# A contrast kernel on one core: the first tile loaded in two pieces instead of three, and stored as one DMA instead of two

## The chip, the cores and the metric

The kernel runs on one core of one Trainium2 chip. The metric is the device time of one execution in microseconds (us), given as the median of several runs. A profile is one more execution, recorded by the hardware profiler; its span runs from the first to the last instruction.

## What is computed

Sixteen images of three 512 x 512 channels in 32-bit floats: 48 channel planes of 262,144 pixels. Each plane is pushed away from its own mean by a factor of 1.5 and clipped.

```
mean = np.mean(x, axis=(2, 3), keepdims=True)
return np.clip(mean + factor * (x - mean), 0, 1).astype(np.float32)
```

With the factor a constant this is `factor * x + (1 - factor) * mean`, clipped to 0 and 1. The input has 50.33 MB, the output as much, so 100.66 MB must cross between HBM and the core's memory.

## The kernel before

**Tiles.** The planes lie one after another in HBM and are cut into rows of 16,384 floats (`ROW`, 64 KB). A tile has 128 such rows, one for each partition, so it holds eight planes of sixteen rows each and 8.39 MB; there are six tiles. The core's memory holds three at a time, in `ring` (L74): tile t lies in slot t mod 3, is worked on in place and stored from there. So tile 3 can be loaded only when tile 0 has been stored, tile 4 after tile 1, tile 5 after tile 2.

**One tile's work** (`compute`, L92). First the sums of the rows, in `add` (L82): VectorE (DVE) reduces the first 4,352 columns (`SUM`) at L85, and ScalarE (ACT) runs over the other 12,032 at L89, copying each element onto itself and accumulating. Then TensorE multiplies these partial sums with `blockw` (L100), a 128 x 128 matrix with (1 - factor) / 262,144 wherever two rows belong to one plane; the result, in `bias`, is the shift of each row. The matmul reads the DVE part and the ACT part one after the other and adds them up; one call in the source is two matmul instructions. Then two passes of DVE: multiply by the factor and add the shift (L103), clip below and above (L106). Then the store (L80).

**Tile 0 is special.** It is loaded in three column pieces: 2,048 columns (`SHORT`, 8 KB of each row), then up to column 8,192 (`HALF`, 24 KB of each row), then the other half (32 KB of each row). Its sums are taken for each half by itself, with 4,352 columns on DVE and 3,840 on ACT in each. Its two DVE passes and its store are cut at column 2,048: the first 8 KB of each row are finished and stored, then the other 56 KB.

**Order.** The order in which each engine gets its instructions is that of the source (`manual_schedule`, L111 to L125): the loads of tiles 0, 1 and 2, the work on tiles 0, 1 and 2 with each one's stores, the loads of tiles 3, 4 and 5, the work on these. Engines run beside each other and wait for data by semaphores. All DMAs are issued by SyncE (SP), which does nothing else, in this order; an issue that must wait holds up those behind it. All DMAs go through one queue that sixteen DMA engines serve, and each row of a DMA is one packet: an engine gets 8 packets of each of these 128-row DMAs, and one small packet that reports completion.

Of the kernel before, what the change touches and what calls it, by code (L numbers as in the profile page):

```python
# [1 line left out]

# [4 lines left out]


P = 128  # L10
ROW = 16384
HALF = ROW // 2
BUFS = 3
SHORT = 2048
SUM = 4352


@with_exitstack
def kernel(
    ctx: ExitStack,  # L20
    tc: tile.TileContext,
    x: bass.AP,
    factor: float,
    out: bass.AP,
):

    nc = tc.nc
    f32 = mybir.dt.float32  # L30
    Alu = mybir.AluOpType
    Act = mybir.ActivationFunctionType

    B, C, H, W = x.shape
    n_img, n_pix = B * C, H * W
    ppi = n_pix // ROW
    per_tile = P // ppi
    n_tiles = n_img // per_tile
    assert ppi * ROW == n_pix and per_tile * n_tiles == n_img

    factor = float(factor)
    wconst = (1.0 - factor) / float(n_pix)

    x_f = x.rearrange("b c h w -> (b c h w)")
    out_f = out.rearrange("b c h w -> (b c h w)")

    def dram(ap, t, c0=0, c1=ROW):
        return bass.AP(tensor=ap.tensor, offset=t * P * ROW + c0, ap=[[ROW, P], [1, c1 - c0]])

    consts = ctx.enter_context(tc.tile_pool(name="consts", bufs=1))  # L50
    xpool = ctx.enter_context(tc.tile_pool(name="xpool", bufs=1))
    small = ctx.enter_context(tc.tile_pool(name="small", bufs=1))
    psum = ctx.enter_context(tc.tile_pool(name="psum", bufs=1, space=bass.MemoryType.PSUM))


    sums = small.tile([P, 4 * n_tiles], f32, name="sums")
    bias = psum.tile([P, n_tiles], f32, name="bias")

    blockw = consts.tile([P, P], f32, name="blockw")
    blocks = blockw.rearrange("p (a b) -> p a b", b=ppi)  # L60
    nc.gpsimd.memset(blockw, wconst)  # L61
    for base, step in ((0, -ppi), (ppi - 1, ppi)):
        nc.gpsimd.affine_select(  # L63
            out=blocks,
            in_=blocks,
            compare_op=Alu.is_ge,
            fill=0.0,
            base=base,
            pattern=[[step, per_tile], [0, ppi]],
            channel_multiplier=1 if step < 0 else -1,  # L70
        )


    ring = xpool.tile([P, BUFS, ROW], f32, name="ring")  # L74

    def load(t, c0=0, c1=ROW):
        nc.sync.dma_start(out=ring[:, t % BUFS, c0:c1], in_=dram(x_f, t, c0, c1))  # L77

    def store(t, c0=0, c1=ROW):
        nc.sync.dma_start(out=dram(out_f, t, c0, c1), in_=ring[:, t % BUFS, c0:c1])  # L80

    def add(t, col, c0, c1, c2):  # L82
        xt = ring[:, t % BUFS, :]
        own = sums[:, 4 * t + col : 4 * t + col + 2]
        nc.vector.tensor_reduce(  # L85
            out=own[:, 0:1], in_=xt[:, c0:c1], axis=mybir.AxisListType.X, op=Alu.add
        )
        part = xt[:, c1:c2]
        nc.scalar.activation(out=part, in_=part, func=Act.Copy, accum_out=own[:, 1:2])  # L89
        return [own[:, 1:2], own[:, 0:1]]  # L90

    def compute(t, *cuts):  # L92
        xt = ring[:, t % BUFS, :]
        if t == 0:
            parts = add(t, 0, 0, SUM, HALF) + add(t, 2, HALF, HALF + SUM, ROW)
        else:
            parts = add(t, 0, 0, SUM, ROW)
        shift = bias[:, t : t + 1]
        for k, part in enumerate(parts):
            nc.tensor.matmul(shift, blockw, part, start=k == 0, stop=k == len(parts) - 1)  # L100
        for c0, c1 in zip((0, *cuts), (*cuts, ROW)):
            part = xt[:, c0:c1]
            nc.vector.tensor_scalar(  # L103
                out=part, in0=part, scalar1=factor, scalar2=shift, op0=Alu.mult, op1=Alu.add
            )
            nc.vector.tensor_scalar(  # L106
                out=part, in0=part, scalar1=0.0, scalar2=1.0, op0=Alu.max, op1=Alu.min
            )
            store(t, c0, c1)

    with tc.manual_schedule():  # L111
        load(0, 0, SHORT)
        load(0, SHORT, HALF)
        load(0, HALF, ROW)
        load(1)
        load(2)
        compute(0, SHORT)
        compute(1)
        compute(2)
        load(3)  # L120
        load(4)
        load(5)
        compute(3)
        compute(4)
        compute(5)  # L125


# [1 line left out]
_INS = ['x', 'factor']  # L129
_OUTS = [((16, 3, 512, 512), 'float32')]  # L130

_NUMBERS = {'factor': 1.5}


# [26 lines left out]
```

## Time and profile before

| | |
|---|---|
| time, median of 3 runs | 239.36 us (239.26 to 239.4) |
| span of the profiled execution | 237.3 us |
| DMA packets, bytes | 2160, 100.66 MB |
| DVE busy | 137.4 us |
| ACT busy | 59.9 us |
| tile 0 sums start (first half, second half) | 12.94 us, 22.58 us |
| tiles 1, 2 have arrived (ACT starts on them) | 41.93 us, 62.40 us |
| stores of tile 0 issued | 30.52 us, 45.83 us |
| stores of tiles 1, 2 issued | 71.00 us, 93.82 us |
| loads of tiles 3, 4, 5 issued | 94.24 us, 101.08 us, 120.82 us |
| tiles 3, 4, 5 have arrived | 139.79 us, 159.21 us, 178.57 us |
| stores of tiles 3, 4, 5 issued | 168.97 us, 191.81 us, 214.64 us |

The profiled execution's own device time is not recorded beside its span; the median of the timed runs lies 239.36 - 237.3 = 2.06 us above it, for what happens before the first and after the last instruction.

In the lines of the profile, L is a line of the kernel, "out<-in" the names of what an instruction writes and reads, and x a count. DVE is VectorE, ACT ScalarE, PE TensorE, SPq the queue of SyncE. The row named DMA has one digit for each of 40 equal slices of the span: the busy share of the sixteen DMA engines in tenths, 9 for 90% or more. A packet counts where it starts, so in a narrow window the share can be far above 1 and in the next one 0.

### The profile page before, as it was taken

How to read it: one execution, taken by the hardware profiler on the slowest of the kernel's cores; microseconds unless marked ns; L12 is line 12 of the kernel's file. 1: busy time of each engine (PE TensorE's matmuls, PEld its weight loads, DVE VectorE, ACT ScalarE, POOL GpSimd, SP SyncE). 2: the span in 40 equal slices, each digit the busy share in tenths (PEclk: the TensorE clock that was granted, in tenths of full speed). 3: DMA queues.
4: the chain of work that ended last, by engine and by line, in shares of the span. 5: the costliest groups of instructions: out<-in, count | busy, mean ns of one | idle time of the engine just before them, and what ended most of it. 6: DMA issues, size and time to landing. Idle time of an engine off the chain costs nothing.

```text
span 237.3 us, 186 instructions
## 1 busy us (share of the span) xinstructions
PE 7.9 (3%) x28; PEld 6.9 (3%) x28; DVE 137.4 (58%) x21; ACT 59.9 (25%) x15; POOL 1.1 (0%) x7
## 2 busy tenths in 40 slices
PE   0010100010001000000000000100000000000000
PEld 0010100010001000000000000100000000000000
DVE  0071899949998998000000043499989998991000
ACT  2051300980492000000000049319509800000000
POOL 1000000000000000000000000000000000000000
DMA  7999989899799798989899998989899998989894
GB/s 289 418 442 442 530 353 530 353 486 398 331 464 454 341 530 353 530 353 519 365 442 442 398 486 353 530 354 530 353 475 409 431 453 376 508 353 530 353 530 177
DMA packets 2160, 100.66 MB, mean 424 GB/s; under 512 B 240, under 2 KB 240, under 8 KB 240
## 3 DMA queue, kind: packets, MB, share of 16 engines
q1 hardware_dynamic: 2160, 100.66, 98.7%
HBM read 50.33 MB, written 50.33 MB: 424 GB/s over the span
## 4 chain that ended last, share of the span: by engine, by line
DVE 43%; DMA 36%; ACT 9%; PE 2%; SPq 1%; issue 0%; DVEq 0%; ACTq 0%
DMA ring<-in_x_dram 36%; DVE ring L103 18%; DVE ring L106 18%; ACT ring L89 9%; DVE sums L85 6%; PE bias L100 2%; SPq L77 1%; SPq L80 0%; DVEq L103 0%; ACTq L89 0%
## 5 line engine op out<-in xcount | busy, mean ns | idle before, releaser
L89 ACT ACTIVATE ring<-ring 128x12032 f32<-128x12032 f32 (+1 forms) x7 | 58.0, 8280 | 128.2 <-DMA ring<-in_x_dram 128.2
L85 DVE TENSOR_REDUCE sums<-ring 128x1 f32<-128x4352 f32 x7 | 32.8, 4683 | 63.9 <-DMA ring<-in_x_dram 63.9
L103 DVE TENSOR_SCALAR ring<-ring,bias 128x16384 f32<-128x16384 f32 (+2 forms) x7 | 52.8, 7538 | 12.9 <-PE bias L100 12.9
L106 DVE TENSOR_SCALAR ring<-ring 128x16384 f32<-128x16384 f32 (+2 forms) x7 | 52.3, 7476 | 0.2
L100 PE MATMUL bias<-sums,blockw 128*128 128x1 f32 x28 | 7.9, 360 | 189.1 <-ACT ring L89 175.4
L100 PEld LDWEIGHTS bias<-sums,blockw 128*128 128x128 f32 x28 | 6.9, 314 | 190.0 <-ACT ring L89 159.4
L89 ACT ACT_TABLE_LOAD x1 | 1.3, 1283 | 0.8 <-PEq L142 0.8
L89 ACT ACTIVATION_READ_ACCUMULATOR ring<-ring 128x1 f32 x7 | 1.3, 187 | 0.0
L63 POOL TENSOR_SCALAR_AFFINE_SELECT blockw<-blockw 128x128 f32<-128x128 f32 x2 | 0.7, 340 | 0.1
L61 POOL MEMSET blockw<- 128x128 f32 x1 | 0.2, 204 | 0.3 <-POOLq L142 0.3
L142 POOL MEMSET const-bfloat16-1.0<- 128x1 bf16 x1 | 0.1, 102 | 0.0
L142 POOL MEMSET const-uint8-127<- 128x1 uint8 x1 | 0.1, 102 | 0.0
L142 POOL MEMSET const-float32-0.0<- 128x1 f32 x1 | 0.1, 98 | 0.3 <-issue 0.3
L142 POOL MEMSET const-float32-1.0<- 128x1 f32 x1 | 0.1, 98 | 0.0
## 6 DMA issues: line engine op xcount, KB each, us to landing
out_dram<-ring SPq DMA_DIRECT2D x1, 7168.0 KB, 35.9
ring<-in_x_dram SPq DMA_DIRECT2D x1, 4096.0 KB, 20.8
ring<-in_x_dram SPq DMA_DIRECT2D x1, 3072.0 KB, 11.6
ring<-in_x_dram SPq DMA_DIRECT2D x1, 1024.0 KB, 4.7
out_dram<-ring SPq DMA_DIRECT2D x1, 1024.0 KB, 34.3
ring<-in_x_dram SPq DMA_DIRECT2D x5, 57.7
out_dram<-ring SPq DMA_DIRECT2D x5, 27.0
```

What stands on the lines that cost most here:

```text
L61: nc.gpsimd.memset(blockw, wconst)
L63: nc.gpsimd.affine_select(out=blocks, in_=blocks, compare_op=Alu.is_ge, fill=0.0, base=base, pattern=[[step, per_tile], [0, ppi]], channel ...
L77: nc.sync.dma_start(out=ring[:, t % BUFS, c0:c1], in_=dram(x_f, t, c0, c1))
L85: nc.vector.tensor_reduce(out=own[:, 0:1], in_=xt[:, c0:c1], axis=mybir.AxisListType.X, op=Alu.add)
L89: nc.scalar.activation(out=part, in_=part, func=Act.Copy, accum_out=own[:, 1:2])
L100: nc.tensor.matmul(shift, blockw, part, start=k == 0, stop=k == len(parts) - 1)
L103: nc.vector.tensor_scalar(out=part, in0=part, scalar1=factor, scalar2=shift, op0=Alu.mult, op1=Alu.add)
L106: nc.vector.tensor_scalar(out=part, in0=part, scalar1=0.0, scalar2=1.0, op0=Alu.max, op1=Alu.min)
L142: nc = _bacc.Bacc("TRN2", target_bir_lowering=False, num_devices=1)
```

## The change

Tile 0 is loaded in two pieces, its two column halves (32 KB of each row each). Its sums are taken as in every other tile: DVE over columns 0 to 4,351, ACT over the other 12,032, which need both halves. Its two DVE passes run over whole rows, and its store is one DMA of whole 64 KB rows. The other tiles keep their instructions, and the order of loads, work and stores stays the same; it is now written as a loop over groups of three tiles. `sums` shrinks from four columns for each tile to two.

```
-    def add(t, col, c0, c1, c2):
+    def add(t, c0, c1, c2):
...
-    def compute(t, *cuts):
+    def compute(t):
         xt = ring[:, t % BUFS, :]
-        if t == 0:
-            parts = add(t, 0, 0, SUM, HALF) + add(t, 2, HALF, HALF + SUM, ROW)
-        else:
-            parts = add(t, 0, 0, SUM, ROW)
+        parts = add(t, 0, SUM, ROW)
...
-        for c0, c1 in zip((0, *cuts), (*cuts, ROW)):
-            part = xt[:, c0:c1]
-            nc.vector.tensor_scalar(
-                out=part, in0=part, scalar1=factor, scalar2=shift, op0=Alu.mult, op1=Alu.add
-            )
-            nc.vector.tensor_scalar(
-                out=part, in0=part, scalar1=0.0, scalar2=1.0, op0=Alu.max, op1=Alu.min
-            )
-            store(t, c0, c1)
+        nc.vector.tensor_scalar(
+            out=xt, in0=xt, scalar1=factor, scalar2=shift, op0=Alu.mult, op1=Alu.add
+        )
+        nc.vector.tensor_scalar(
+            out=xt, in0=xt, scalar1=0.0, scalar2=1.0, op0=Alu.max, op1=Alu.min
+        )
 
     with tc.manual_schedule():
-        load(0, 0, SHORT)
-        load(0, SHORT, HALF)
-        load(0, HALF, ROW)
-        load(1)
-        load(2)
-        compute(0, SHORT)
-        compute(1)
-        compute(2)
-        load(3)
-        load(4)
-        load(5)
-        compute(3)
-        compute(4)
-        compute(5)
+        for first in range(0, n_tiles, BUFS):
+            turn = range(first, min(first + BUFS, n_tiles))
+            for t in turn:
+                if t == 0:
+                    load(t, 0, HALF)
+                    load(t, HALF, ROW)
+                else:
+                    load(t)
+            for t in turn:
+                compute(t)
+                store(t)
```

More of the change, by code (lines that the diff above doesn't have):

```diff
@@ L11 @@
 ROW = 16384
+BUFS = 3
+SUM = 4352
 HALF = ROW // 2
-BUFS = 3
-SHORT = 2048
-SUM = 4352
 @with_exitstack
@@ L53 @@
     psum = ctx.enter_context(tc.tile_pool(name="psum", bufs=1, space=bass.MemoryType.PSUM))
-    sums = small.tile([P, 4 * n_tiles], f32, name="sums")
+    sums = small.tile([P, 2 * n_tiles], f32, name="sums")
     bias = psum.tile([P, n_tiles], f32, name="bias")
@@ L80, in store @@
         nc.sync.dma_start(out=dram(out_f, t, c0, c1), in_=ring[:, t % BUFS, c0:c1])
-    def add(t, col, c0, c1, c2):
+    def add(t, c0, c1, c2):
         xt = ring[:, t % BUFS, :]
-        own = sums[:, 4 * t + col : 4 * t + col + 2]
+        own = sums[:, 2 * t : 2 * t + 2]
         nc.vector.tensor_reduce(
```

## The prediction

> **What bounds the kernel now.** I read the page first, for the share of each engine, then the DMA slices.
>
> ```profile
> span 237.3 us, 186 instructions
> PE 7.9 (3%) x28; PEld 6.9 (3%) x28; DVE 137.4 (58%) x21; ACT 59.9 (25%) x15; POOL 1.1 (0%) x7
> DMA  7999989899799798989899998989899998989894
> DMA packets 2160, 100.66 MB, mean 424 GB/s; under 512 B 240, under 2 KB 240, under 8 KB 240
> q1 hardware_dynamic: 2160, 100.66, 98.7%
> ```
>
> No compute engine is busy for more than 58% of the span, while the one DMA queue fills 98.7% of sixteen DMA engines' time; only the first and last slices are low. The chain of work puts 43% on DVE, but that chain steps from release to release and does not ask whether the queue was empty meanwhile. It was not: the five loads are issued within 3.3 us of the start, and each store is issued before the transfers ahead of it have drained. The timeline gives the issue of a store and the DMA view its time to landing; the second half shows the thinnest leads. Store 3 is issued at 168.97, while load 5 lands at 178.57 (ACT's start, by the timeline): lead 9.6 us. Store 5 is issued at 214.64, while store 4 lands at 191.81 + 25.3 = 217.1: lead 2.5 us. So time is bytes over DMA rate, plus a start, plus whatever slows a packet.
>
> Therefore I looked at packets, with the stage table on narrow windows. It counts a packet in the window in which it starts, so share x width is the mean packet time when exactly one packet per engine starts in the window (GB/s x width shows this: 2097 x 0.50 us = 16 x 64 KB).
>
> ```profile
> core 0: us, PE busy (x) PEld busy (x) DVE busy (x) ACT busy (x) POOL busy (x), PEclk, DMA share, GB/s
> 55.50:56.00 0.50, 0.00 (x0) 0.00 (x0) 0.50 (x1) 0.00 (x0) 0.00 (x0) 1.00 4.84 2097
> 57.90:58.40 0.50, 0.00 (x0) 0.00 (x0) 0.50 (x1) 0.00 (x0) 0.00 (x0) 1.00 7.06 2097
> 58.40:61.30 2.90, 0.00 (x0) 0.00 (x0) 2.90 (x1) 0.00 (x0) 0.00 (x0) 1.00 0.00 0
> 172.50:173.25 0.75, 0.00 (x0) 0.00 (x0) 0.75 (x1) 0.00 (x0) 0.00 (x0) 1.00 3.23 1398
> 174.90:175.65 0.75, 0.00 (x0) 0.00 (x0) 0.75 (x1) 0.00 (x0) 0.00 (x0) 1.00 3.39 1398
> ```
>
> An ordinary 64 KB packet takes 4.84 x 0.50 = 2.42 us. The sixteen that start at 57.9 to 58.4 take 7.06 x 0.50 = 3.53 us: **1.11 us lost on all engines at once**, with no new packet for 2.9 us. They are the last packets of load 2, right before the queue turns from loads to stores. The same place in the second half, the last packets of load 5 (row 174.90), shows 3.39 x 0.75 = 2.54 against 3.23 x 0.75 = 2.42 us: only 0.12 lost. Landings say the same: tile 2 arrives 62.40 - 41.93 = 20.47 us after tile 1, tile 5 only 178.57 - 159.21 = 19.36 after tile 4. What differs: the first turn meets stores of 8 KB and 56 KB rows, issued at 30.52 and 45.83; the second meets a store of 64 KB rows, issued 9.6 us ahead.
>
> **The change, part by part.**
>
> *Packets.* Thirteen DMAs replace fifteen. By windows of one packet size: 8 KB 1.03 x 0.30 = 0.309 us, 24 KB 1.82 x 0.50 = 0.910, 32 KB 2.43 x 0.50 = 1.215, 56 KB 3.02 x 0.70 = 2.114. One engine carries 8 rows of a tile: the load goes from 8 x (0.309 + 0.910 + 1.215) to 8 x 2 x 1.215, or 19.47 to 19.44; the store from 8 x (0.309 + 2.114) = 19.38 to 8 x 2.42 = 19.36. Two completion packets per engine go too (9 ns each in the packet records). Together -0.05 - 0.02, rounding included about -0.1 us, all on the path.
>
> Here the Trainium skill, "DMA: Bandwidth & Descriptors", section "Anatomy of one DMA — SWDGE (gpsimd) path", gives a DMA about 2.0 us fixed plus its bytes over 436 GB/s, for the other descriptor path. By it two fewer DMAs would save 4 us where nothing overlaps; this trace disagrees, since the 8 KB-row store lands at 30.52 + 34.3 = 64.82, 2.42 us after tile 2, which is its 8 x 0.309 = 2.47.
>
> *The start.* The first packets go from 8 KB to 32 KB. The records show the first sixteen, from 1.82 us on, taking 2.19 x 0.38 = 0.83 us instead of 0.309, a start cost of 0.52. It looks like the wait for first data, which 32 KB pays once also. I take 0; bounds -0.5 (it vanishes) and +0.5 (paid twice).
>
> *The load-to-store turn at 58 us.* It gets what the turn at 175 us has: 64 KB rows behind it, one store queued about 10 us ahead. If these set the loss, it falls from 1.11 to 0.12: -0.99. Bounds: 0 (stall stays) and -1.11 (goes entirely). I take -0.99, since the row at 174.90 is the near one in packet size, queue depth and lead, while the row at 57.90 has only "first turn of the run" in common.
>
> *Compute of tile 0.* DVE loses one sum (4.69) and its four passes 1.29 + 1.23 + 7.68 + 7.63 = 17.83 become 8.76 + 8.70 = 17.46. ACT's two of 3.40, of which the second starts at 22.58, become one of 10.23 that must wait for the whole row; eight matmuls become four. The chain behind tile 0 is then that of tile 3: store 3 is issued 168.97 - 139.79 = 29.2 us after its tile arrives, and the next two 22.84 and 22.83 later. Tile 0 arrives at about 22.5, so the stores would be issued at 51.7, 74.5 and 97.4 instead of 30.52 with 45.83, 71.00 and 93.82. The cover is the queue: without the stall loads drain at 61.3, then stores 0 and 1 at about 80.6 and 100.0 (19.35 each). Leads: 9.6, 6.1, 2.6 us. Store 5 ran with 2.5, and the engines went from store 4 to store 5 without a gap, so this costs 0; if the cover were gone, each us of lateness beyond it would cost a us.
>
> *SP's queue.* It issues in program order, still store 2 then load 3 (0.33 and 0.54 us). Load 3 moves from 94.24 to about 97.8, and is due when store 2 drains at about 119.4, so 21 us remain. Loads 4 and 5 wait, as now, for stores 1 and 2 to land (SP waits 25.6 us for them, with a tile queued behind each). No wait is added. Behind load 5 all is unchanged.
>
> *Sum*, against the profiled execution: span 237.3 - 0.1 - 0.99 = 236.2. The median of the timed runs is 239.36, which is 2.06 above that span, so I take 239.36 - 1.1 = **238.3 us**. That carries over an assumption: that the timed runs, which differ by only 0.14, hold the stall that the profile holds.
>
> **The rivals.**
>
> *Stall stays.* It may come with the first write of a run, or only under the profiler, or be a chance event. Then only packets count: 239.36 - 0.1 = 239.3. For it: there is one stall in one execution, and two of these causes I cannot exclude. Against: outside the start and the turns the 64 KB packets stay at 2.42, so a chance event would have had to pick one slot in some 97; and a cold write should lengthen the first store packets, yet these take 0.309, the usual time for 8 KB.
>
> *Fixed cost per DMA.* If each DMA cost some 2 us of its own on the path, two fewer give 239.36 - 4 = 235.4. The landing 2.42 us after tile 2 leaves no room for that. The page named above is its source.
>
> *Turn gets worse, slower.* If the engine holds back the last load packet while it fetches what follows, a 64 KB row behind it could cost a whole packet more, 2.42 us instead of 1.11: 239.36 + 1.3 - 0.1 = 240.6. It decides from a stall of about 1.7 us on (1.11 + 0.1 + 0.2% of 239). Against: the turn at 175 us has 64 KB rows and loses 0.12.
>
> *Third store late, slower.* Store 2 has 2.6 us of lead; from an issue to its first packets the run's start shows 1.82 - 0.80 = 1.0, so 1.6 are spare. If tile 0's DVE sum ran after ACT's instead of beside it, everything would slide by 4.69 and the queue would stand empty 3.1 us: 238.3 + 3.1 = 241.4. Against: tiles 3 to 5 do the same work and DVE and ACT start 0.14 us apart.
>
> **How the numbers follow.** Stall goes: 0.56, 238.3, own range 238.0 to 238.7. Stall stays: 0.34, 239.3. Fixed cost: 0.02. The two slower ones: 0.05 and 0.03. A measurement of this kernel tells about 0.2% (0.48 us) from no change. So faster 0.58, same 0.34, slower 0.08. The range of 8 in 10 must take in both likely cases with the start's bounds on the upper: 238.0 to 239.6; it leaves out the fixed cost, the slower pair and some of the tails.
>
> **What would show it.** The stage table around 57 to 61 us of the new trace: last packets of load 2 near 2.5 us, tile 2 some 19.4 us after tile 1, load 3 landing about 1.1 us earlier than 139.79. Stores issued near 51.7, 74.5 and 97.4, and packets back to back from 61 to 101. DMA packets 2160 - 2 x 144 = 1872. I am wrong if the last packets of load 2 still take 3.5 us (stall stays), take more (turn worse), or if no packet starts for over 2.5 us around 100 (late store); and if the trace loses the stall while the timed runs do not move, the stall was the profiler's.

## The result

The changed kernel takes 239.88 us (median of 20 runs, 239.59 to 241.69) against 239.42 us for the kernel before (239.26 to 239.87, 20 runs beside it). The ratio is 1.0023, with a 95% interval of 1.0014 to 1.0033: **slower by about 0.46 us**, where 1.1 us faster was forecast.

The profiled execution is one of the slower ones, 240.79 us. In every run that lists both, the time is 1.7 to 1.8 us above the span (here 240.79 - 239.0). So the profile of before, with its span of 237.3, stands for about 239.1 us, a little below the fastest of these 20 runs, and the two pages are further apart than the kernels are.

### The profile page after: what moved, and what is told of

Read it like the earlier page. It is cut to its first block, busy times and chain, and to the rows that moved or that the text cites. A ratio compares the mean times of both kernels' runs of the same rounds, so it can differ in the third digit from the quotient of the medians.

```text
span 239.0 us, 168 instructions
## 1 busy us (share of the span) xinstructions
PE 6.7 (3%) x24; PEld 5.9 (2%) x24; DVE 132.5 (55%) x18; ACT 63.2 (26%) x13; POOL 1.1 (0%) x7
## 2 busy tenths in 40 slices
DMA packets 1872, 100.66 MB, mean 421 GB/s; under 512 B 208, under 2 KB 208, under 8 KB 208
## 3 DMA queue, kind: packets, MB, share of 16 engines
q1 hardware_dynamic: 1872, 100.66, 98.6%
## 4 chain that ended last, share of the span: by engine, by line
DVE 52%; DMA 26%; ACT 9%; PE 2%; issue 1%; SPq 0%; DVEq 0%; ACTq 0%
DMA ring<-in_x_dram 26%; DVE ring L97 22%; DVE ring L100 22%; ACT ring L88 9%; DVE sums L84 8%; PE bias L96 2%; ACT L88 1%; SPq L76 0%; SPq L79 0%; DVEq L97 0%; ACTq L88 0%
## 5 line engine op out<-in xcount | busy, mean ns | idle before, releaser
L88 ACT ACTIVATE ring<-ring 128x12032 f32<-128x12032 f32 x6 | 61.4, 10230 | 104.2 <-DMA ring<-in_x_dram 104.2
L97 DVE TENSOR_SCALAR ring<-ring,bias 128x16384 f32<-128x16384 f32 x6 | 52.5, 8758 | 27.8 <-PE bias L96 27.8
L84 DVE TENSOR_REDUCE sums<-ring 128x1 f32<-128x4352 f32 x6 | 28.1, 4681 | 54.5 <-DMA ring<-in_x_dram 54.5
L100 DVE TENSOR_SCALAR ring<-ring 128x16384 f32<-128x16384 f32 x6 | 52.2, 8694 | 0.2
L96 PE MATMUL bias<-sums,blockw 128*128 128x1 f32 x24 | 6.7, 360 | 190.7 <-ACT ring L88 169.5
L96 PEld LDWEIGHTS bias<-sums,blockw 128*128 128x128 f32 x24 | 5.9, 315 | 191.4 <-ACT ring L88 135.1
L88 ACT ACT_TABLE_LOAD x1 | 1.3, 1283 | 23.1 <-DMA ring<-in_x_dram 23.1
```

What stands on the lines that cost most here:

```text
L84: nc.vector.tensor_reduce(out=own[:, 0:1], in_=xt[:, c0:c1], axis=mybir.AxisListType.X, op=Alu.add)
L97: nc.vector.tensor_scalar(out=xt, in0=xt, scalar1=factor, scalar2=shift, op0=Alu.mult, op1=Alu.add)
L100: nc.vector.tensor_scalar(out=xt, in0=xt, scalar1=0.0, scalar2=1.0, op0=Alu.max, op1=Alu.min)
```

## The profile after

The page of the changed kernel, the lines that answer to those shown of before:

```profile
span 239.0 us, 168 instructions
PE 6.7 (3%) x24; PEld 5.9 (2%) x24; DVE 132.5 (55%) x18; ACT 63.2 (26%) x13; POOL 1.1 (0%) x7
DMA  7999989899898999989898989999899998989894
DMA packets 1872, 100.66 MB, mean 421 GB/s; under 512 B 208, under 2 KB 208, under 8 KB 208
q1 hardware_dynamic: 1872, 100.66, 98.6%
```

288 packets fewer, less DVE work, and still one queue that is full to 98.6%. The time is again in the packets. The stage table, in windows in which exactly one 64 KB packet of each engine starts (the last two columns are DMA share and GB/s; share x width is the mean time of one packet): the last packets of load 2, of store 2 and of load 5, which are the three places where the queue turns between loads and stores. Kernel before:

```profile
57.95:58.40 0.45, 0.00 (x0) 0.00 (x0) 0.45 (x1) 0.00 (x0) 0.00 (x0) 1.00 7.85 2330
116.95:117.65 0.70, 0.00 (x0) 0.00 (x0) 0.00 (x0) 0.00 (x0) 0.00 (x0) 1.00 3.45 1498
174.90:175.65 0.75, 0.00 (x0) 0.00 (x0) 0.75 (x1) 0.00 (x0) 0.00 (x0) 1.00 3.39 1398
```

Kernel after:

```profile
58.30:58.90 0.60, 0.33 (x2) 0.24 (x2) 0.16 (x1) 0.00 (x0) 0.00 (x0) 1.00 5.49 1748
117.20:117.70 0.50, 0.00 (x0) 0.00 (x0) 0.00 (x0) 0.00 (x0) 0.00 (x0) 1.00 5.62 2097
175.70:176.10 0.40, 0.00 (x0) 0.00 (x0) 0.40 (x1) 0.00 (x0) 0.00 (x0) 1.00 8.57 2621
```

Before: 7.85 x 0.45 = 3.53, 3.45 x 0.70 = 2.42, 3.39 x 0.75 = 2.54 us. After: 5.49 x 0.60 = 3.29, 5.62 x 0.50 = 2.81, 8.57 x 0.40 = 3.43. The stall at 58 us, which was to go, is still there; the two later turns, which were to stay cheap, now cost 0.39 and 1.01 us over the ordinary 2.42.

One more row was not foreseen. The timeline around the arrival of tile 0, after:

```profile
13.34 4.68 DVE L84 TENSOR_REDUCE sums<-ring 128x1 f32<-128x4352 f32 x1 [13.34 <-DMA ring<-in_x_dram]
23.06 1.28 ACT L88 ACT_TABLE_LOAD   x1 [23.06 <-DMA ring<-in_x_dram]
24.35 10.23 ACT L88 ACTIVATE ring<-ring 128x12032 f32<-128x12032 f32 x1
```

ACT's table load (the instruction that stands ahead of ACT's first operation) was here in the kernel before:

```profile
0.80 1.28 ACT L89 ACT_TABLE_LOAD   x1 [0.80 <-PEq L142]
```

Now it waits for tile 0 and sits between its arrival and its sum. SP's queue shows what follows:

```profile
53.46 46.02 SPq L79 DMA_DIRECT2D out_dram<-ring  x3
99.14 0.33 SPq L79 DMA_DIRECT2D out_dram<-ring  x1
99.53 21.69 SPq L76 DMA_DIRECT2D ring<-in_x_dram  x3
101.14 0.34 SPq L76 DMA_DIRECT2D ring<-in_x_dram  x1
```

Store 0 is issued at 53.46 instead of the forecast 51.7 (1.28 us of it is the table load; most of the rest is that tile 0 arrived at 23.06 instead of 22.5 in this execution). The third store goes out at 99.14 instead of 97.4, and store 1 lands at 101.14, when the second of these loads is issued. The lead of store 2 over the end of the work queued before it has shrunk to 2.0 us, from 7.3 in the kernel before.

## The experiments

In the expectations, the time of before is taken as 239.4 and that of after as 239.9. Unless another base is named, each edit is made to the changed kernel. Kernels of one group ran on one chip beside the kernel before. Where an edit writes to `spare`, that is a scratch tile that nothing reads.

### First group: the first packets, or late stores?

The profile of after has slow first packets (about 2.2 us for 32 KB), so the first theory blamed these.

**e1: tile 0 loaded in the old three pieces.**

```
-                    load(t, 0, HALF)
+                    load(t, 0, 2048)
+                    load(t, 2048, HALF)
```

> The changed kernel with the first tile loaded in the old three pieces (8, 24, 32 KB per row). Theory 'first packet': the first packet of each DMA engine pays a fetch time that grows with its size (8 KB: 0.83 - 0.31 = 0.52 us in the trace of before, 32 KB: about 2.2 - 1.21 = 0.98 in the trace of after), so this one is back at the time before, 239.4 us, with tile 0 complete at about 22.6. Rival 'late stores' (tile 0's store issued at 53.5 instead of 30.5, as one DMA, makes the turns from loads to stores and back dearer): it stays at the time after, 239.9.

Measured: 239.72 us, ratio 1.0013 (1.0001 to 1.0024). The old load does not bring the old time back.

**e2: the kernel before, tile 0 loaded in two halves.**

```
-        load(0, 0, SHORT)
-        load(0, SHORT, HALF)
+        load(0, 0, HALF)
```

> The kernel before with only the load changed: tile 0 in two halves, its store still in two DMAs and issued early. 'First packet': 239.9 us, tile 0 complete at about 23.0. 'Late stores': 239.4, as before, since both stores go out as early as before.

Measured: 239.38 us, ratio 0.9998 (0.999 to 1.0007). The new load costs nothing. "First packet" has fallen twice.

**e3: tile 0 loaded by one DMA.**

```
-                    load(t, 0, HALF)
-                    load(t, HALF, ROW)
+                    load(t)
```

> The changed kernel with tile 0 loaded by one DMA of 64 KB rows. 'First packet': through 0.52 at 8 KB and 0.98 at 32 KB a straight line gives about 1.6 us at 64 KB, so 0.6 over the changed kernel: 240.5 us, first packets of about 4.0 us. If the start cost did not grow beyond 32 KB, 239.9. 'Late stores': DVE's sum of tile 0 starts 10 us later but still beside ACT's, so stores are issued as in the changed kernel and the time is 239.9.

Measured: 239.71 us, ratio 1.0018 (1.0001 to 1.0035). That is below what either theory gave. "First packet" with a cost that grows (240.5) is out; but "late stores" does not explain it either, since the stores were not late: the table load is at 0.80, where ACT's first operation waits for one DMA, stores 0 and 2 go out at 51.81 and 97.46, and the later turns take 2.42 and 2.70 us.

**e4: an early table load.**

```
+    early = small.tile([P, 1], f32, name="early")
+    nc.gpsimd.memset(early, 0.0)
+    nc.scalar.activation(out=early, in_=early, func=Act.Copy)
```

> The changed kernel with a small extra activation ahead of the first tile, so that ACT's table load (1.28 us, at 23.06 in the trace of after, at 0.80 before) is over when tile 0 arrives. Stores of tiles 0 to 2 are then issued about 1.3 us earlier (52.2, 75.0, 97.9). 'First packet': no change against the changed kernel, 239.9 us, since the queue is never empty. 'Late stores': some or all of the loss comes back, towards 239.4.

Measured: 239.33 us, ratio 0.9996 (0.9988 to 1.0004). **The whole loss is gone**, with the load in halves and the store as one DMA. Its table load, its store 2, and the stage table at the three turns:

```profile
0.79 1.28 ACT L75 ACT_TABLE_LOAD   x1 [0.79 <-PEq L136]
97.37 0.33 SPq L83 DMA_DIRECT2D out_dram<-ring  x1
57.90:58.40 0.50, 0.00 (x0) 0.00 (x0) 0.50 (x1) 0.00 (x0) 0.00 (x0) 1.00 7.33 2097
117.05:117.70 0.65, 0.00 (x0) 0.00 (x0) 0.00 (x0) 0.00 (x0) 0.00 (x0) 1.00 3.72 1613
175.05:175.70 0.65, 0.00 (x0) 0.00 (x0) 0.65 (x1) 0.00 (x0) 0.00 (x0) 1.00 4.00 1613
```

3.67, 2.42 and 2.60 us: the later turns are as cheap as in the kernel before.

### Second group: the lateness, or the table load itself?

**e5: e3 with e4's early operation.**

> The changed kernel with tile 0 loaded by one DMA (that took 239.71 us) and a small extra ACT operation at the start. With one DMA the table load already sits at 0.80 us, so the stores go out as before this edit (51.8, 74.6, 97.5). If an early first operation of ACT is what mends (theory 'ACT starts late'): 239.35. If 64 KB first packets or the load's shape cost something of their own: 239.7 stays.

Measured: 239.71 us, ratio 1.0015 (1.0006 to 1.0024). One DMA of 64 KB rows for tile 0 costs 0.3 us of its own, with store 2 issued at 97.57 and cheap later turns (2.42 and 2.64 us); that isn't in the change and stays open.

**e6: e4, and 1.3 us of ACT copying ahead of tile 0's sum.**

```
+        if t == 0:
+            nc.scalar.activation(out=spare, in_=xt[:, HALF : HALF + 1344], func=Act.Copy)
```

> The changed kernel with the table load early (that took 239.33 us) and then 1.3 us of extra ACT copying put ahead of tile 0's sum, so that the stores go out as late as in the changed kernel (about 53.2, 76.0, 98.9) with no table load amid the loads. Theory 'late stores': 239.8. Theory 'table load amid the stream': 239.35.

Measured: 239.87 us, ratio 1.0019 (1.001 to 1.0028). No table load amid the loads, and the loss is back.

**e7: e4, and three more table loads where ACT is idle.**

```
+        if t == 0:
+            for k, func in enumerate((Act.Exp, Act.Sqrt, Act.Exp, Act.Sqrt)):
+                nc.scalar.activation(out=spare[:, k : k + 1], in_=early, func=func)
```

> The changed kernel with the first table load early (239.33 us) and three more table loads at about 33 to 40 us, where ACT is idle and the loads stream; the stores go out at 51.7, 74.5, 97.4. 'Table load amid the stream': 239.8 for one disturbance, up to 240.7 for three. 'Late stores': 239.35.

Measured: 239.41 us, ratio 1.0007 (0.9998 to 1.0015). Three table loads at 33 to 37 us, and next to no loss: it is the lateness.

**e8: the changed kernel again.**

> The changed kernel itself, beside the others on one chip, for a second profile. Its time again about 0.46 us over the kernel before. If the first profile is typical, the last packets before the second turn from loads to stores (about 176 us) again take 3.4 us and those before the turn to loads (about 117) 2.8; if these losses come and go from execution to execution, they differ from 1.0 and 0.5 us.

Measured: 239.91 us, ratio 1.0019 (1.001 to 1.0028). The stage table of its profile:

```profile
57.90:58.45 0.55, 0.31 (x2) 0.22 (x2) 0.13 (x1) 0.00 (x0) 0.00 (x0) 1.00 6.66 1907
117.15:117.70 0.55, 0.00 (x0) 0.00 (x0) 0.00 (x0) 0.00 (x0) 0.00 (x0) 1.00 4.61 1907
175.35:175.90 0.55, 0.00 (x0) 0.00 (x0) 0.55 (x1) 0.00 (x0) 0.00 (x0) 1.00 5.75 1907
```

3.66, 2.54 and 3.16 us: both later turns are dear again, by less. The slow first packets did not come again (its packets of the first 4 us lose 0.60 us per engine by the packet records, against 1.03 in the first profile of after and 0.59 in that of before).

### Third group: which store, how late, and the first turn

**e9: e4, and a DVE operation ahead of tile 2's passes.**

```
+        if t == 2:
+            nc.vector.tensor_scalar(
+                out=spare, in0=xt[:, :2048], scalar1=0.0, scalar2=1.0, op0=Alu.max, op1=Alu.min
+            )
```

> The changed kernel with the table load early (239.33 us), and 1.3 us of extra DVE work ahead of tile 2's two passes only: stores 0 and 1 go out early (51.7, 74.5), store 2 and the load behind it late (98.7, 99.1). Theory 'third store late' (it is store 2 and load 3, issued 2 us instead of 3.8 before store 1 lands, that cost): 239.85, with packets of over 2.42 us at about 117 and a dear turn at about 176. Rival 'all three late' (the first turn or the whole chain pays): 239.4.

Measured: 239.43 us, ratio 1.0001 (0.9991 to 1.001). The edit failed to do what it was for: the operation ran mostly in the gap in which DVE awaits the matmul, and store 2 went out at 97.91, only 0.5 us later than in e4. It says that a lead of 3.25 us is enough for cheap turns. Its profiled execution took 239.95 us, 0.5 over the median, although its turns cost no more than in e4: by the packet records its sixteen engines end within 1.29 us of each other, against 0.54 in e4. So engines that drift apart are a second way to lose time, which these stage rows do not show.

**e10: e6 with the copying three times.**

> The changed kernel with the table load early and 3.9 us of extra ACT copying ahead of tile 0's sum: stores at about 55.7, 78.5 and 101.4. 'Third store late': store 2 is now issued about when store 1 lands, so the queue is empty for the about 1.0 us from issue to first packet and a little more: 241 to 241.5 us, with a gap at about 101. If a late store 2 costs a fixed 0.5 us whatever the lateness: 239.9.

Measured: 243.16 us, ratio 1.0153 (1.014 to 1.0167), 1.7 us above the upper end of what was expected. The stage table, from the last packets of store 1 on:

```profile
97.90:98.60 0.70, 0.00 (x0) 0.00 (x0) 0.70 (x1) 0.00 (x0) 0.00 (x0) 1.00 3.45 1498
98.60:102.35 3.75, 0.00 (x0) 0.00 (x0) 2.87 (x1) 0.00 (x0) 0.00 (x0) 1.00 0.00 0
102.35:102.60 0.25, 0.00 (x0) 0.00 (x0) 0.00 (x0) 0.00 (x0) 0.00 (x0) 1.00 9.98 4194
119.35:119.55 0.20, 0.00 (x0) 0.00 (x0) 0.00 (x0) 0.00 (x0) 0.00 (x0) 1.00 15.70 5243
178.00:178.50 0.50, 0.00 (x0) 0.00 (x0) 0.50 (x1) 0.00 (x0) 0.00 (x0) 1.00 7.07 2097
```

No packet starts for 3.75 us, though one takes 2.42: here the queue did run dry (1.8 us for an engine on average, by the packet records). And the two turns behind it take 15.70 x 0.20 = 3.14 and 7.07 x 0.50 = 3.54 us, 0.72 and 1.12 too much: the gap is paid once, and lateness once more at each later turn.

**e11: e4, and a small store at the start, through ACT's queue.**

```
+        nc.scalar.dma_start(out=dram(out_f, 5, 0, 128), in_=blockw)
```

> The changed kernel with the table load early (239.33 us) and one more DMA at the start, 64 KB from blockw to the head of tile 5's output rows (overwritten by its store later), on ACT's queue. If the 1.1 to 1.3 us that every profile shows in the last packets ahead of the first turn from loads to stores belongs to the first write of a run, it is paid at the start beside the first loads and the time falls to about 238.3. If it belongs to the turn itself: 239.4 to 239.6, the loss at 58 us unchanged.

Measured: 239.56 us, ratio 1.0003 (0.9993 to 1.0012). The small store landed 13.7 us after its issue, long before the turn, and the last packets of load 2 still take 3.54 us: the stall at 58 us is not the cost of the run's first write. A first write through SP's own queue was not tried and is not excluded.

**e12: another share of the sums.**

```
-SUM = 4352
+SUM = 2816
```

> The changed kernel, its late table load kept, with DVE's share of each row sum cut from 4352 to 2816 columns and ACT's grown to 13568. ACT needs 1.3 us more for each tile, DVE 1.65 less: stores of tiles 0 to 2 at about 54.3, 75.5 and 96.6, so the first is later than in the changed kernel and the third 2.3 us earlier. 'Third store late': 239.4, like before. 'All three late': 239.9 or more.

Measured: 239.58 us, ratio 1.0007 (0.9998 to 1.0016); stores at 54.34, about 75.6 and 96.82. Store 0 later than in the changed kernel, store 2 earlier, and most of the loss is gone, though the interval does not tell it from all of it.

### Fourth group: the third store alone, and more turns

**e13: e4, and e9's operation between the two passes of tile 2.**

> The changed kernel with the table load early (239.33 us), and 1.25 us of extra DVE work between the two passes of tile 2: stores 0 and 1 at 51.7 and 74.5 as there, store 2 at about 98.6 and load 3 behind it. 'Third store late': 239.75, packets above 2.42 us at about 117 and a turn at about 176 that costs 0.5 to 0.8. 'All three late': 239.35.

Measured: 239.96 us, ratio 1.0018 (1.001 to 1.0027). Store 0 goes out at 51.91. Store 2, the landing of store 1 (the issue of load 4), and the stage table:

```profile
98.86 0.33 SPq L84 DMA_DIRECT2D out_dram<-ring  x1
101.33 0.34 SPq L81 DMA_DIRECT2D ring<-in_x_dram  x1
57.85:58.60 0.75, 0.00 (x0) 0.00 (x0) 0.75 (x1) 0.00 (x0) 0.00 (x0) 1.00 4.92 1398
117.05:117.90 0.85, 0.00 (x0) 0.00 (x0) 0.00 (x0) 0.00 (x0) 0.00 (x0) 1.00 3.08 1234
175.45:176.05 0.60, 0.00 (x0) 0.00 (x0) 0.60 (x1) 0.00 (x0) 0.00 (x0) 1.00 5.37 1748
```

3.69, 2.62 and 3.22 us: **the third store alone, with load 3 right behind it, brings the whole pattern**, in time and in packets. It is not the extra operation as such: e9 has the same one, ahead of the passes and so without the lateness, and loses nothing.

**e15: the kernel before, and that operation four times.**

> The kernel before, with 4 x 1.25 us of extra DVE work between the two passes of tile 2: the first tile's load, its split store and store 1 as before (30.5, 45.8, 71.0), store 2 at about 98.8 instead of 93.8. 'Third store late': 239.85. 'All three late', or the split store as such: 239.4.

Measured: 241.62 us, ratio 1.0092 (1.0079 to 1.0105): late as in e13 (98.82), in a kernel with the old load and the old split store, but dearer, by 1.8 us more than expected. Its turns take 3.70, 2.93 and 3.07 us. The rest is that its sixteen engines drift apart: the last packets of load 5 start within 1.55 us of each other (0.75 before), and the slowest engine ends the kernel. Why more than in e13 stays open.

**e14: load 3 ahead of store 2.**

```
         store(1)
+        load(3)
         compute(2)
         store(2)
```

> The changed kernel (table load late) with load 3 issued ahead of store 2: loads 0 to 2, stores 0 and 1, load 3, store 2, loads 4 and 5, stores 3 to 5, so five turns instead of three. Load 3 is issued at about 82 when store 0 has landed, so store 2, issued at 98.7, has 20 us of lead. If every turn costs about 1.1 us like the first: 241 or more; if turns are cheap as long as the queue is well filled (0 to 0.2 us, as at 117 and 176 in the early kernels): 239.4 to 239.8.

Measured: 240.02 us, ratio 1.0034 (1.0017 to 1.005). By the packet records the five turns lose 1.09, 0.03, 0.19, 0.03 and 0.27 us. Turns as such are cheap; the first one is not. Here the table load and the lateness of stores 0 and 1 were kept, so its other 0.3 us over before are not placed; in its profile the slowest engine ends 0.67 us after the mean of the sixteen, against 0.30 before.

### The kernels by the lead of store 2

Lead: from the issue of store 2 to the landing of store 1, which is when SP issues load 4. e14 is left out, since its load 3 stands ahead of store 2. The three packet times are means at the three turns, worked out as above.

| kernel | store 2 issued | lead | load 2 | store 2 | load 5 | time |
|---|---|---|---|---|---|---|
| e2 | 93.81 | 7.5 | 3.70 | 2.42 | 2.44 | 239.38 |
| before | 93.82 | 7.3 | 3.53 | 2.42 | 2.54 | 239.4 |
| e12 | 96.82 | 4.3 | 3.53 | 2.42 | 2.68 | 239.58 |
| e3 | 97.46 | 3.9 | 3.66 | 2.42 | 2.70 | 239.71 |
| e4 | 97.37 | 3.8 | 3.67 | 2.42 | 2.60 | 239.33 |
| e7 | 97.42 | 3.8 | 3.74 | 2.42 | 2.43 | 239.41 |
| e11 | 97.64 | 3.7 | 3.54 | 2.42 | 2.49 | 239.56 |
| e5 | 97.57 | 3.5 | 3.46 | 2.42 | 2.64 | 239.71 |
| e9 | 97.91 | 3.25 | 3.60 | 2.42 | 2.59 | 239.43 |
| e1 | 98.52 | 2.6 | 3.75 | 2.45 | 2.94 | 239.72 |
| e13 | 98.86 | 2.5 | 3.69 | 2.62 | 3.22 | 239.96 |
| e8 = after | 98.72 | 2.45 | 3.66 | 2.54 | 3.16 | 239.91 |
| e15 | 98.82 | 2.4 | 3.70 | 2.93 | 3.07 | 241.62 |
| e6 | 98.79 | 2.25 | 3.40 | 2.61 | 3.20 | 239.87 |
| after | 99.14 | 2.0 | 3.29 | 2.81 | 3.43 | 239.88 |
| e10 | 101.55 | under 0 | 3.67 | 3.14 | 3.54 | 243.16 |

In the packets of the two later turns, the step lies between 3.25 and 2.6 us of lead. The times follow it with two exceptions: e3 and e5 are slow with cheap turns (the 64 KB rows of tile 0), and e15 is slower than its turns. The step lies a little above the length of one packet, 2.42 us, so a store issued with less comes when engines are on the last packet they have. What the engine then does differently is not shown: in the changed kernel packets run back to back at 101 us, and the loss appears 16 and 75 us later. Load 3 goes out 0.4 us behind store 2 in all these kernels, and load 4 at the end of the lead, so whether the store, the load behind it or its distance from load 4 counts is not told apart.

The Trainium skill, "DMA: Bandwidth & Descriptors", section "Rules for kernel authors", has a rule to issue a DMA early, compute, and wait for it late, so that its fixed setup cost overlaps. e10 agrees: its store 2, issued at 101.55 behind a queue that had run out, has its first packets at 102.35. The loss at leads of 2.0 to 2.6 us is another one, since no gap stands at 101 us there.

## Why the prediction was wrong

**The step that failed first: "The load-to-store turn at 58 us … it falls from 1.11 to 0.12".** It fell in no kernel. All profiles show 0.87 to 1.33 us there, with a store of 8 KB or of 64 KB rows behind the loads, with stores queued early or late, and with a write through another queue beforehand (e11). The rival "stall stays" was right on this. Of its three causes, chance is out, and so is the first write as far as e11 goes; the profiler is unlikely, as profiled executions are no slower than the others (e1: 239.52 us, within 239.38 to 240.72). What all have in common is that it is the first turn of the run; the cause stays open. The error was to reason from two turns in one execution: the row at 174.90 seemed to be the rule and that at 57.90 the exception that packet size explains, and no second row told size from place.

**The step that made the sign wrong: "Compute of tile 0 … Leads: 9.6, 6.1, 2.6 us. Store 5 ran with 2.5 … so this costs 0".** Two things failed in it. The chain behind tile 0 was not that of tile 3: ACT's table load, 1.28 us, came into it. In these kernels it is early when ACT's first sum waits for one DMA (before, e2, e3: 0.80 us) and late when its columns come from two (after, e1: 22 to 23 us), and the change makes them come from two. The Trainium skill, "ScalarE: Activation LUTs", section "Step-by-step: what each stage is for", says that a table load stands right before the ACTIVATE that needs it, and its figure of 1283 ns under "What ACT_TABLE_LOAD costs" is the 1.28 of these traces. And 2.5 us of lead is not free: store 5 has no turn behind it, so its row could not show a cost that falls due at later turns. The two failed steps also meet: the forecast lead of 2.6 counted on the stall being gone. With the stall, a store issued as forecast has 3.8 us of lead, and e4, which is that kernel (51.69 and 97.37 against the forecast 51.7 and 97.4), loses nothing; the table load takes the lead to 2.45 and 2.0.

**"Third store late, slower"** got 0.03, and is the mechanism. Its place was right, its price (a queue that runs dry) is that of e10, and its threshold was too low: it was put at 1.0 us of lead, and the loss begins between 3.25 and 2.6.

**Packets and the start** were small as forecast. 1872 packets came; e2 and e4, with the new load and e4 also the new store, are within 0.1% of before. So what the diff says in words, load and store of tile 0, costs nothing that these runs can tell; and no run brought the forecast gain.

**The range**, 238.0 to 239.6, excluded 239.88 because lateness had 0.03. Carrying the median 2.06 us above the span was off too: it is 1.7 to 1.8, and the profile of before was an execution 0.3 us faster than its median.

No version beat the kernel before: e4 has the simpler code of the change and the old time, 239.33 against 239.38 beside it.

## What to carry to other kernels

In a kernel that one DMA queue bounds, ask of every issue how long before the end of the work queued ahead of it it comes; here 3.25 us was enough and 2.6 or less too late, and the price did not show at that place but at later turns between loads and stores. Changing the pieces of a load changes how many DMAs the first instruction of an engine waits for, and with it what stands behind that wait, a table load for one; a dummy operation at the start takes it out. Two places in one profile that differ in several ways prove nothing on which of them matters: a second profile of the same kernel is cheap.

## What was not expected of the hardware

The first turn from loads to stores cost 0.87 to 1.33 us in every profile, while later ones cost 0 to 0.28 in the kernels whose store 2 had over 3 us of lead. Its cause stays open; the row size of the store behind it and a first write through another queue are ruled out.

A late DMA of 8.39 MB made engines slower 75 us afterwards (packets of 3.16 to 3.43 us instead of 2.42 at 175 us) with no gap in between that the trace shows.

Table loads followed each other at 33.05, 34.55 and 36.06 us in e7 with a 0.20 us operation between, so one costs 1.28 us here and next to nothing beyond. The Trainium skill, "ScalarE: Activation LUTs", section "What ACT_TABLE_LOAD costs", adds a drain of about 1.38 us, which these rows do not show.
